# Mixer B's class maxima moved behind the window maxima, and a paired write of the class outputs

## The chip, the cores and the metric

One core of a Trainium2 chip runs the whole layer. The metric is the device time of one execution in microseconds (us). The engines are TensorE (PE: matmuls; PEld: its weight loads), VectorE (DVE), ScalarE (ACT), GpSimd (POOL) and SyncE (SP), which issues most of the DMAs. Each engine works off its own list of instructions in order, and semaphores hold an instruction until what it needs is there.

## The reference

The layer is an encoder layer in float32 over 1024 tokens of width 1024: a norm, an input projection, two attention mixers side by side, an output projection with a residual, a mixture of 32 experts (two for each token), and a last norm. The change touches mixer B alone. It has 8 heads of 64 elements, and merges three patterns by their softmax denominators:

```python
DILATED_PATTERNS = ((128, 1), (512, 4), (2048, 16))
for window, dilation in DILATED_PATTERNS:
    o, lse = _dilated_window(q, k, v, window, dilation)   # |key - query| <= window/2, in steps of dilation
    outs.append(o); lses.append(lse)
w = jax.nn.softmax(jnp.stack(lses, axis=0), axis=0)
o = jnp.einsum('pbhs,pbhsd->bhsd', w, jnp.stack(outs, axis=0))
```

Merging by denominators is one softmax over all keys of the three patterns, in which a key that lies in two of them counts twice. So the kernel needs one maximum for each query over everything that it sees.

## The kernel before

**Stages.** The profiled execution runs through: norm, input projection and mixer A (0 to 430 us); mixer B with the first half of the output projection (430 to 663); the second half with the router (to 760); the experts (to 1340); the last norm. Weights are split into a high and a low float32r part and multiplied in three products.

**Mixer B's two kinds of keys.** The second and third pattern together see every key of the query's residue class modulo 4: four classes of 256 tokens. The first pattern sees a window: for each block of 128 tokens a window of 256. Masks are added to the scores and hold the double counts as log 2.

**A head's preparation** (`prepare_b`, L634). `flipped` transposes the head's keys into `k2` [128 x 1024] and the queries into `q2` and, ordered by class, `q2c`, all of them high part over low part. Then come the class maxima (L651 to 658: for each class two matmuls of `q2c` against `k2[:, c::4]`, which is every fourth column of `k2`; VectorE adds the mask and takes the maximum into `mc`, L657), a multiplication that spreads them (`mx`, L663), and the window maxima (L665 to 677, from `q2` against 256 neighbouring columns of `k2`, into `mw`, L676). Between the second and the third pair of windows, at j0 == 4, ScalarE copies the keys into class order (`k2c`, 128 x 1024, written from `by_class(k2)`) and SyncE copies the low half to `k1c` (L669). At the end four small matmuls with `back_m` (L681) bring the class maxima back into token order, five small VectorE instructions (L683 to 688) join the two and write the negative maximum into the query tile `q` (`keep10` in the order below), and eight transposes (L312, 66 rows) make `q1`, which ScalarE evicts and which every score matmul of the head needs.

**A head's attention** (`steps_b`, L693) has eight steps: four classes (`front_c`: scores, L714 and L715; `back_c`: values, L727 to 730, two classes in one PSUM bank) and four pairs of windows (`front_w`, L740 and L741; `back_w`, L768 to 770). `masked` adds the mask (VectorE, L700), takes the exponential (`p`, ScalarE), rounds it (`ph`, ScalarE) and subtracts (`pl`, GpSimd). After every second class ScalarE evicts the bank into the head's output tile `ob` (L732), class by class, every fourth column; VectorE adds the window parts (L772, three for each head), and `divided` transposes (L749) and divides.

**What sets the order.** `attend` (L464) makes the next head's preparation a generator, and advances it three times after each of the eight steps, so 24 times for each head; a `yield` in `prepare_b` is one advance. This is the program's order. The scheduler of the framework then orders each engine's list anew by a time model of its own, so a moved line moves its neighbours too. `k2c` and `k1c` exist once: the next head's copy can only be written when `front_c` of all four classes of the current head is through. PSUM has three banks for `x` (transposes and maxima), two for `b` (scores), and `i0` and `i1` in turn for outputs. `first_half` (L841) runs beside the heads: its matmuls (L837, 192 of 512 columns in all) are work that PE can do while a head waits; in the prediction they are the fill.

Of the kernel before, what the change touches and what calls it, by code (L numbers as in the profile page):

```python
# [13 lines left out]
F32 = mybir.dt.float32  # L14
# [5 lines left out]
OP = mybir.AluOpType  # L20
AX = mybir.AxisListType

P = 128
# [7 lines left out]
NEG = -1e30  # L31
# [22 lines left out]
def _window(j):  # L54

    return min(max(128 * j - 64, 0), S - 256)
# [70 lines left out]
def tile_encoder(ctx, tc, I, out):  # L127
    nc = tc.nc
    V, A, G, T = nc.vector, nc.scalar, nc.gpsimd, nc.tensor

    def act(o, i, f=AF.Copy, **kw):
        A.activation(o, i, f, **kw)  # L132
# [26 lines left out]
    def bank(tag, shape, dt=F32, name=None):  # L159
        tag = next(turn) if tag == "ip" else names.get(tag, tag)  # L160
        pool, n = psum[tag]
        return pool.tile(shape, dt, tag=tag, name=name or f"ps_{tag}", bufs=n)
# [136 lines left out]
    def by_class(t):  # L299

        return t.rearrange("p (i c) -> p c i", c=4)

    def classes(t):

        return t.rearrange("p (c i) -> p c i", c=4)

    def flipped(dst, src, rows, classed=None):

        for b in range(2):
            ps = bank("x", [P, 4, P], F32R)  # L310
            for i in range(4):
                T.transpose(ps[:rows, i], src[:, 4 * b + i], eyer)  # L312
            if classed is not None:
                act(classes(classed[:rows])[:, :, 128 * b:128 * b + 128],
                    by_class(ps[:rows].rearrange("p j i -> p (j i)")))
            if dst is not None:
                act(dst[:rows, 512 * b:512 * b + 512].rearrange("p (j i) -> p j i", j=4), ps[:rows])
            yield
# [61 lines left out]
    for j in range(NT):  # L380
        x, ss, _ = rows_x[j]
# [6 lines left out]
        for b in range(2):  # L388
            ps = bank("x", [P, 4, P])
# [205 lines left out]
    k1c = k1c[0:66]  # L595
# [6 lines left out]
    qst2 = attb.enter_context(tc.tile_pool(name="qst2", bufs=2, side="right"))  # L602
    pp2 = attb.enter_context(tc.tile_pool(name="pp2", bufs=2, side="right"))
    masks = mcon.tile([P, 6, 256], F32, name="masks")
    mask_c, mask_w = masks[:, 0:2], masks[:, 2:6]
    back_m = mcon.tile([P, 4, P], F32, name="back")
    own = small[:, 60:64]
# [10 lines left out]
    def load_v(h, what):  # L618

        for part in range(2 if h < 8 else 0):  # L620
            to, hs = slice(65 * part, 65 * part + 64), slice(64 * h, 64 * h + 64)
            if what == "w":
                nc.sync.dma_start(v_w[:, :, to].bitcast(F32), bv_d[part, :, hs].rearrange("(j p) c -> p j c", p=P))
            else:
                for c in range(4):
                    nc.sync.dma_start(v_c[:, c, :, to].bitcast(F32),
                                      bv_d[part, c::4, hs].rearrange("(t i) d -> i t d", t=2))

    def load_b(h):
        if h < 8:  # L630
            nc.sync.dma_start(k_st.bitcast(F32), bk_d[h])
            nc.sync.dma_start(q_st[h % 2][:, :, 0:192].bitcast(F32), bq_d[h])

    def prepare_b(h, _):  # L634
        k, q = k_st, q_st[h % 2]
        if h == 0:
            load_b(0)
            nc.sync.dma_start(masks, I["masks"])
            nc.sync.dma_start(back_m, I["back"])
            load_v(0, "c")  # L640
            for _ in range(IDLE):
                yield
        k2 = k2s[h % 2]
        yield from flipped(k2, k, P)
        k1 = k1s[h % 2]
        nc.sync.dma_start(k1[0:64].bitcast(F32), k2[64:128].bitcast(F32))
        q2c = q2s[h % 2]
        yield from flipped(q2, q[:, :, 0:128], P, q2c)
        load_b(h + 1)
        mc = qst2.tile([P, 4, 2], F32, name="mc")  # L650
        junk = qst2.tile([P, 256], F32, name="junk", bufs=1)  # L651
        for c in range(4):
            ps = bank("x", [P, 2, 256])
            for t in range(2):
                T.matmul(ps[:, t], q2c[:, 256 * c + P * t:256 * c + P * t + P], k2[:, c::4], start=True, stop=True)
            for t in range(2):
                V.tensor_tensor_reduce(junk, ps[:, t], mask_c[:, t], 1.0, NEG, op0=OP.add, op1=OP.max,  # L657
                                       accum_out=mc[:, c, t:t + 1])
            yield
        mw = qst2.tile([P, NT], F32, name="mw")  # L660

        mx = qst2.tile([P, 4, 4, 2], F32, name="mx")
        V.tensor_tensor(mx, mc[:, :, None, :].to_broadcast([P, 4, 4, 2]),  # L663
                        own[:, None, :, None].to_broadcast([P, 4, 4, 2]), op=OP.mult)
        for j0 in range(0, NT, 2):  # L665
            if j0 == 4:

                act(classes(k2c), by_class(k2))
                nc.sync.dma_start(k1c[0:64].bitcast(F32), k2c[64:128].bitcast(F32))  # L669
            ps = bank("x", [P, 2, 256])  # L670
            for t in range(2):
                w0 = _window(j0 + t)
                T.matmul(ps[:, t], q2[:, P * (j0 + t):P * (j0 + t) + P], k2[:, w0:w0 + 256], start=True, stop=True)
            for t in range(2):
                w = 0 if j0 + t == 0 else 3 if j0 + t == NT - 1 else 1
                V.tensor_tensor_reduce(classes(junk), by_class(ps[:, t]), classes(mask_w[:, w]), 1.0, NEG,  # L676
                                       op0=OP.add, op1=OP.max, accum_out=mw[:, j0 + t:j0 + t + 1])
            yield
        pm = bank("x", [P, 4, 2])
        for c in range(4):  # L680
            T.matmul(pm, back_m[:, c], mx[:, c], start=(c == 0), stop=(c == 3))  # L681
        m = qst2.tile([P, NT], F32, name="m")
        V.tensor_copy(m.rearrange("p (t i) -> p t i", t=2), pm.rearrange("p i t -> p t i"))  # L683
        t = qst2.tile([P, NT], F32, name="negm")
        V.tensor_tensor(m, m, mw, op=OP.max)
        V.tensor_scalar(t, m, -1.0, None, op0=OP.mult)
        V.tensor_copy(q[:, :, 192], t)
        V.tensor_tensor(q[:, :, 193], t, q[:, :, 192], op=OP.subtract)
        q1 = qst2.tile([66, S], F32R, name="q1")
        yield  # L690
        yield from flipped(None, q[:, :, 128:194], 66, q1)
        return k2, k1, q2c, q1

    def steps_b(h, state):
        k2, k1, q2, q1 = state
        st = {}
# [21 lines left out]
        def back_c(c):  # L718
            if c == 0:
                st["o"] = pp2.tile([65, S], F32, name="ob", bufs=1)  # L720
            if c % 2 == 0:
                st["po"] = bank("ip", [P, 2, 256])
            po, cc = st["po"], c % 2
            ph, pl = st["c", c]
            for t in range(2):
                ts = slice(256 * t, 256 * t + 256)
                T.matmul(po[0:65, cc], v_c[:, c, t, 0:65], ph[:, ts], start=(cc == 0 and t == 0), stop=False,  # L727
                         skip_group_check=True)
                T.matmul(po[0:64, cc], v_c[:, c, t, 65:129], ph[:, ts], start=False, stop=False, skip_group_check=True)
                T.matmul(po[0:65, cc], v_c[:, c, t, 0:65], pl[:, ts], start=False, stop=(t == 1), skip_group_check=True)  # L730
            if cc:
                act(st["o"].rearrange("p (i c) -> p c i", c=4)[:, c - 1:c + 1], po[0:65])  # L732

        def front_w(j0):
            if j0 == NT - 2:
# [20 lines left out]
        def back_w(j0):  # L756
# [16 lines left out]
            if j0 == NT - 2:  # L773
                for b in range(2):
                    divided(b)

        return [(lambda c=c: front_c(c), lambda c=c: back_c(c)) for c in range(4)] + \
            [(lambda j=j: front_w(j), lambda j=j: back_w(j)) for j in range(0, NT, 2)]

# [391 lines left out]
    def load_rows(rows):  # L1171

        gathers.append(G.indirect_dma_start(out=x_g, out_offset=None, in_=xn_d[:, :],  # L1173
                                            in_offset=bass.IndirectOffsetOnAxis(ap=rows, axis=0),
                                            bounds_check=S - 1, oob_is_err=False).ins)
        return x_g
# [7 lines left out]
    def rows_in(xg):  # L1184

        st = {"g": bank("b", [P, 512]), "u": bank("c", [P, 512])}
        for b in range(2):
            st["x", b] = bank("a", [P, 4, P])
            for k in range(4):
                T.transpose(st["x", b][:, k], xg[:, (4 * b + k) * P:(4 * b + k + 1) * P], eye)  # L1190
        return st
# [68 lines left out]
    with tc.manual_schedule(engines={mybir.EngineType.PE}):  # L1260
# [6 lines left out]
        st = rows_in(xg)  # L1267
        rows_split(st, 0)
        for e in range(NE):
# [14 lines left out]
            st = coming  # L1284
# [38 lines left out]
    with tc.For_i(0, n, 1) as i:  # L1323
# [13 lines left out]
        st = rows_in(load_rows(rows[:, 0:1]))  # L1337
# [39 lines left out]
```

## Time and profile before

| | us |
|---|---|
| three runs | 1385.99, 1386.30, 1390.66 |
| median | 1386.3 |
| the profiled execution | 1382.04 |
| its span from the first to the last instruction | 1380.4 |
| PE busy in the span | 1287.7 (93%) |
| DVE busy | 1160.4 (84%) |
| ACT busy | 941.9 (68%) |
| POOL busy | 570.5 (41%) |

A busy PE is not PE at its peak: a matmul's time runs from its start to the end of its results, and the next one starts before that. So how close matmuls follow each other is read from start to start. [...]

### The profile page before, as it was taken

What the parts mean: (1) busy time and instruction counts of PE and PEld (TensorE: products, weight loads), DVE (VectorE), ACT (ScalarE), POOL (GpSimd) and SP (SyncE); (2) the same over time, 40 slices, a digit from 0 to 9 for tenths busy, and PEclk for the clock granted to TensorE, in tenths of its full rate; (3) what the DMA queues carried; (4) which work ended last, traced back from release to release, by engine and by line L of the source; (5) the groups of instructions that cost most, each with busy time, mean ns of one, the idle gap of its engine ahead of it and who ended that gap; (6) DMA issues with size and microseconds to landing.
All of it is one profiled execution on the core that took longest, in us unless ns stands there. A gap on an engine that the chain in (4) does not pass through costs nothing. (4 is left out here: it accounts for less than half of the span.)

```text
span 1380.4 us, 22002 instructions
## 1 busy us (share of the span) xinstructions
PE 1287.7 (93%) x7333; PEld 1091.4 (79%) x7333; DVE 1160.4 (84%) x2001; ACT 941.9 (68%) x1390; POOL 570.5 (41%) x557
## 2 busy tenths in 40 slices
PE   5999999999998988999897999999999999999983
PEld 5999788888976877888686788878888888888862
DVE  6788997899868777887687899989999999999976
ACT  5334566655666885776443888878888888888873
POOL 5673566746566563546354611112111111111215
PEclk9999999999999999999997999999999999999997
DMA  7113321222242485567757999999999999999935
GB/s 260 62 39 85 77 69 57 67 59 49 51 135 61 123 182 149 119 145 234 287 189 266 339 373 364 350 344 360 345 368 342 354 353 358 354 347 351 361 92 224
DMA packets 213685, 301.73 MB, mean 219 GB/s; under 512 B 94436, under 2 KB 116068, under 8 KB 213569
## 3 DMA queue, kind: packets, MB, share of 16 engines
q1 hardware_dynamic: 201168, 275.01, 59.5%
q0 software_dynamic: 11968, 24.55, 6.7%
q8 instruction: 58, 0.95, 0.3%
q10 hardware_dynamic: 432, 0.75, 0.3%
q14 instruction: 59, 0.48, 0.1%
HBM read 267.85 MB, written 44.58 MB: 226 GB/s over the span
## 5 line engine op out<-in xcount | busy, mean ns | idle before, releaser
L1173 POOL DMA_INDIRECT o_b<-xn_d,rows x32 | 51.4, 1606 | 323.8 <-PE ps_a L1190 321.1
L141 DVE TENSOR_TENSOR wl<-unit,wh 128x1024 fp32r<-128x1024 f32 x130 | 156.3, 1221 | 19.9 <-ACT wh L132 19.1
L264 PE MATMUL ps_i<-wih,ul 128*128 128x256 f32 x576 | 164.5, 286 | 1.4 <-DVE ul L141 1.4
L262 PE MATMUL ps_i<-wih,uh 128*128 128x256 f32 x576 | 164.1, 285 | 0.9 <-ACT uh L132 0.8
L263 PE MATMUL ps_i<-wil,uh 128*128 128x256 f32 x576 | 163.4, 284 | 0.0
L542 POOL TENSOR_TENSOR psum<-psum,p 128x512 f32<-128x512 f32 x93 | 136.1, 1463 | 63.2 <-ACT p L132 54.8
L132 ACT ACTIVATE wh<-unit 128x1024 fp32r<-128x1024 f32 x130 | 136.6, 1062 | 34.7 <-PE ps_b L1206 12.5
L132 ACT ACTIVATE ph<-p 128x512 fp32r<-128x512 f32 x192 | 118.6, 633 | 12.0 <-DVE pl L458 5.7
L458 DVE TENSOR_TENSOR pl<-p,ph 128x512 fp32r<-128x512 f32 x93 | 98.3, 1057 | 23.9 <-ACT ph L132 23.7
L132 ACT ACTIVATE p<-ps_b 128x512 f32<-128x512 f32 x128 | 74.9, 596 | 62.1 <-PE ps_b L532 39.1
L262 PEld LDWEIGHTS ps_i<-wih,uh 128*128 128x128 f32 x576 | 111.0, 193 | 7.3 <-ACT uh L132 1.7
L263 PEld LDWEIGHTS ps_i<-wil,uh 128*128 128x128 f32 x576 | 110.9, 193 | 5.7
L264 PEld LDWEIGHTS ps_i<-wih,ul 128*128 128x128 f32 x576 | 111.0, 193 | 5.3 <-DVE ul L141 1.9
L705 POOL TENSOR_TENSOR pl<-p,ph 128x512 fp32r<-128x512 f32 x64 | 86.5, 1365 | 64.3 <-ACT ph L132 57.1
L141 DVE TENSOR_TENSOR wl<-rawc,wh 128x1024 fp32r<-128x1024 f32 x80 | 96.3, 1221 | 11.0 <-ACT wh L132 10.0
L132 ACT ACTIVATE wh<-rawc 128x1024 fp32r<-128x1024 f32 x80 | 84.4, 1062 | 20.8 <-PE ps_b L1206 8.7
L1243 POOL DMA_INDIRECT y_d<-y,rows x31 | 49.9, 1611 | 115.6 <-ACT y L132 112.3
L513 DVE TENSOR_REDUCE m<-ps_x 128x1 f32<-128x512 f32 x128 | 84.8, 678 | 7.9 <-PE ps_x L512 7.6
L1206 PE MATMUL ps_b<-wh,x_hi 128*128 128x512 f32 x256 | 86.5, 419 | 0.0
L1230 PE MATMUL ps_d<-wh,h_hi 128*128 128x512 f32 x256 | 81.0, 397 | 1.7 <-ACT h_hi L132 1.7
L1230 PE MATMUL ps_d<-wh,h_lo 128*128 128x512 f32 x256 | 81.1, 398 | 1.5 <-DVE h_lo L141 1.5
L1206 PE MATMUL ps_b<-wl,x_hi 128*128 128x512 f32 x256 | 81.3, 399 | 0.0
(323 smaller groups left out, 3864.1 us busy)
## 6 DMA issues: line engine op xcount, KB each, us to landing
unit<-in_w_up SPq DMA_DIRECT2D x47, 512.0 KB, 11.8
unit<-in_w_gate SPq DMA_DIRECT2D x42, 512.0 KB, 12.2
unit<-in_w_down SPq DMA_DIRECT2D x41, 512.0 KB, 12.1
rawc<-in_w_gate SPq DMA_DIRECT2D x30, 512.0 KB, 12.1
rawc<-in_w_down SPq DMA_DIRECT2D x26, 512.0 KB, 12.1
rawc<-in_w_up SPq DMA_DIRECT2D x24, 512.0 KB, 11.7
h_b<-in_w_down SPq DMA_DIRECT2D x19, 512.0 KB, 12.8
raw<-in_w_in SPq DMA_DIRECT2D x36, 256.0 KB, 2.9
```

Of the source, the lines that this page charges most:

```text
L132: A.activation(o, i, f, **kw)
L141: (eng or V).tensor_tensor(lo, src, hi, op=OP.subtract)
L262: T.matmul(ps[:, jj], u_hi[j][:, k], wh, start=(k == 0 and jj == 0), stop=False, skip_group_check=True)
L263: T.matmul(ps[:, jj], u_hi[j][:, k], wl, start=False, stop=False, skip_group_check=True)
L264: T.matmul(ps[:, jj], u_lo[j][:, k], wh, start=False, stop=(k == 7), skip_group_check=True)
L458: engine("pl").tensor_tensor(pl, p, ph, op=OP.subtract)
L513: V.tensor_reduce(m2[:, j, b:b + 1], ps, axis=AX.X, op=OP.max)
L542: engine("s").tensor_tensor(st["s"], st["s"], p, op=OP.add)
L705: G.tensor_tensor(pl, p, ph, op=OP.subtract)
L1173: gathers.append(G.indirect_dma_start(out=x_g, out_offset=None, in_=xn_d[:, :], in_offset=bass.IndirectOffsetOnAxis(ap=rows, axis=0), boun ...
L1206: T.matmul(st["gu"[n % 2]], lhs[:, k % 4], rhs[:, 512 * a:512 * a + 512], start=(k == 0 and i == 0), stop=(k == 7 and i == 2))
L1230: T.matmul(py[b], lhs[:, k], w[n][:, 512 * b:512 * b + 512], start=(k == 0 and i == 0), stop=(k == 3 and i == 2))
```

## The change

The window maxima come first. Then, for all heads but the first, the generator gives three advances away, so that the copy into `k2c` still stands behind the current head's last class in the program. Then come the copy and its DMA, and after them the class maxima, which now read 256 neighbouring columns of `k2c` and no longer every fourth of `k2`. `mx` comes after them. No arithmetic is added or taken away, and every engine has as many instructions as before. The eviction of two classes (`act(st["o"]...)`) writes, for each token of the class, both classes' values next to each other, and reads PSUM in that order: in turn from one class's half of the bank and from the other's.

```diff
         mc = qst2.tile([P, 4, 2], F32, name="mc")
         junk = qst2.tile([P, 256], F32, name="junk", bufs=1)
-        for c in range(4):
-            ps = bank("x", [P, 2, 256])
-            for t in range(2):
-                T.matmul(ps[:, t], q2c[:, 256 * c + P * t:256 * c + P * t + P], k2[:, c::4], start=True, stop=True)
-            for t in range(2):
-                V.tensor_tensor_reduce(junk, ps[:, t], mask_c[:, t], 1.0, NEG, op0=OP.add, op1=OP.max,
-                                       accum_out=mc[:, c, t:t + 1])
-            yield
         mw = qst2.tile([P, NT], F32, name="mw")
-
-        mx = qst2.tile([P, 4, 4, 2], F32, name="mx")
-        V.tensor_tensor(mx, mc[:, :, None, :].to_broadcast([P, 4, 4, 2]),
-                        own[:, None, :, None].to_broadcast([P, 4, 4, 2]), op=OP.mult)
         for j0 in range(0, NT, 2):
-            if j0 == 4:
-
-                act(classes(k2c), by_class(k2))
-                nc.sync.dma_start(k1c[0:64].bitcast(F32), k2c[64:128].bitcast(F32))
             ps = bank("x", [P, 2, 256])
             ...
             yield
+
+        for _ in range(3 if h else 0):
+            yield
+        act(classes(k2c), by_class(k2))
+        nc.sync.dma_start(k1c[0:64].bitcast(F32), k2c[64:128].bitcast(F32))
+        for c in range(4):
+            ps = bank("x", [P, 2, 256])
+            for t in range(2):
+                T.matmul(ps[:, t], q2c[:, 256 * c + P * t:256 * c + P * t + P], k2c[:, 256 * c:256 * c + 256],
+                         start=True, stop=True)
+            for t in range(2):
+                V.tensor_tensor_reduce(junk, ps[:, t], mask_c[:, t], 1.0, NEG, op0=OP.add, op1=OP.max,
+                                       accum_out=mc[:, c, t:t + 1])
+            yield
+
+        mx = qst2.tile([P, 4, 4, 2], F32, name="mx")
+        V.tensor_tensor(mx, mc[:, :, None, :].to_broadcast([P, 4, 4, 2]),
+                        own[:, None, :, None].to_broadcast([P, 4, 4, 2]), op=OP.mult)
         pm = bank("x", [P, 4, 2])
...
             if cc:
-                act(st["o"].rearrange("p (i c) -> p c i", c=4)[:, c - 1:c + 1], po[0:65])
+                act(st["o"].rearrange("p (i c) -> p i c", c=4)[:, :, c - 1:c + 1],
+                    po[0:65].rearrange("p c i -> p i c"))
```

The lists of the engines move at three places. In the rows below the number behind a name is that of the buffer: `keep2` is `k2c`, `keep7` the next head's `k2`, `keep8` its `q2c`, `keep1` its `q2`, `keep10` the query tile. The lines of the changed kernel are two or three higher.

**PE in the middle of a head's attention** (the head whose transposes start at 563.5 us), around the first two classes' values, before:

```order
L655 MATMUL ps_x_7007<-keep7_5006,keep8_5007 128x256 x2
L727 MATMUL ps_i0_6995<-ph_6884,v_c_5022 65x256
L729 MATMUL ps_i0_6995<-ph_6884,v_c_5022 64x256
L673 MATMUL ps_x_7015<-keep7_5006,keep1_5000 128x256 x2
L730 MATMUL ps_i0_6995<-pl_6886,v_c_5022 65x256
L727 MATMUL ps_i0_6995<-ph_6884,v_c_5022 65x256
L729 MATMUL ps_i0_6995<-ph_6884,v_c_5022 64x256
L730 MATMUL ps_i0_6995<-pl_6886,v_c_5022 65x256
L727 MATMUL ps_i0_6995<-ph_6926,v_c_5022 65x256
```

and in the changed kernel (L657 is now the window maxima, L671 the class maxima, L832 the fill's transposes):

```order
L657 MATMUL ps_x_7008<-keep7_5006,keep1_5000 128x256 x2
L729 MATMUL ps_i0_6996<-ph_6884,v_c_5022 65x256
L731 MATMUL ps_i0_6996<-ph_6884,v_c_5022 64x256
L832 MATMUL ps_x_7026<-mats_60,on_7018 128x128 x4
L732 MATMUL ps_i0_6996<-pl_6886,v_c_5022 65x256
L729 MATMUL ps_i0_6996<-ph_6884,v_c_5022 65x256
L731 MATMUL ps_i0_6996<-ph_6884,v_c_5022 64x256
L732 MATMUL ps_i0_6996<-pl_6886,v_c_5022 65x256
L671 MATMUL ps_x_7054<-keep2_5001,keep8_5007 128x256 x2
L729 MATMUL ps_i0_6996<-ph_6926,v_c_5022 65x256
```

The first pair of class maxima now stands between the first class's values and the second's, where the second pair's maxima need the copy `keep2`; the eight maxima ahead of the values are now the window's.

**ACT from the eviction of `q1` to the copy `k2c`** in the same head, before:

```order
L132 ACTIVATE p_6881<-p_6881 128x512
L132 ACTIVATE keep8_5007<-ps_x_6956 128x4x128
L132 ACTIVATE keep1_5000<-ps_x_6956 128x512
L132 ACTIVATE p_6923<-p_6923 128x512
L132 ACTIVATE ph_6884<-p_6881 128x512
L132 ACTIVATE keep2_5001<-keep7_5006 128x1024
L132 ACTIVATE p_6987<-p_6987 128x512
L132 ACTIVATE ph_6926<-p_6923 128x512
```

and in the changed kernel:

```order
L132 ACTIVATE p_6881<-p_6881 128x512
L132 ACTIVATE keep8_5007<-ps_x_6956 128x4x128
L132 ACTIVATE keep1_5000<-ps_x_6956 128x512
L132 ACTIVATE p_6923<-p_6923 128x512
L132 ACTIVATE ph_6884<-p_6881 128x512
L132 ACTIVATE p_6988<-p_6988 128x512
L132 ACTIVATE keep2_5001<-keep7_5006 128x1024
L132 ACTIVATE ph_6926<-p_6923 128x512
```

The copy stands one exponential later, and the rounding of the second class (`ph_6926`) comes right behind it.

**DVE at the end of that head**, where the next head's maximum is made, before:

```order
L683 COPY m_7104<-ps_x_7099 128x8
L676 ISA junk_6966,mw_7012<-ps_x_7071,masks_5019 128x256
L676 ISA mw_7012 128x1
L685 TENSOR_TENSOR m_7104<-m_7104,mw_7012 128x8
L686 TENSOR_SCALAR negm_7106<-m_7104 128x8
L687 CAST keep10_5009<-negm_7106 128x8
L688 TENSOR_TENSOR keep10_5009<-negm_7106,keep10_5009 128x8
L772 TENSOR_TENSOR ob_6994<-ob_6994,ps_i0_7161 65x4x112
L864 TENSOR_TENSOR h_b_6008<-ps_d_7570,x2_7389 128x512
L772 TENSOR_TENSOR ob_6994<-ob_6994,ps_i1_7195 65x4x128
L772 TENSOR_TENSOR ob_6994<-ob_6994,ps_i0_7258 65x4x80
```

and in the changed kernel:

```order
L679 TENSOR_TENSOR mx_7119<-mc_6965,mats_60 128x32
L867 TENSOR_TENSOR h_b_6001<-ps_d_7570,x2_7372 128x512
L685 COPY m_7126<-ps_x_7121 128x8
L775 TENSOR_TENSOR ob_6995<-ob_6995,ps_i0_7161 65x4x112
L687 TENSOR_TENSOR m_7126<-m_7126,mw_6967 128x8
L775 TENSOR_TENSOR ob_6995<-ob_6995,ps_i1_7195 65x4x128
L688 TENSOR_SCALAR negm_7128<-m_7126 128x8
L689 CAST keep10_5009<-negm_7128 128x8
L775 TENSOR_TENSOR ob_6995<-ob_6995,ps_i0_7258 65x4x80
L690 TENSOR_TENSOR keep10_5009<-negm_7128,keep10_5009 128x8
```

All three window additions into `ob` now stand ahead of the last instruction of the maximum, where before they stood behind it.

## Rows read from the trace of the kernel before

**Rows 1.** The page, busy time: engine, us, share of the span, instructions.

```profile
PE 1287.7 (93%) x7333; PEld 1091.4 (79%) x7333; DVE 1160.4 (84%) x2001; ACT 941.9 (68%) x1390; POOL 570.5 (41%) x557
```

**Rows 2.** Busy time by windows: from:to, length, PE, PEld, DVE, ACT, POOL, PEclk, DMA, GB/s.

```profile
428.00:660.00 232.00, 211.42 (x1404) 183.88 (x1404) 180.95 (x500) 161.14 (x274) 125.71 (x121) 0.94 0.57 144
...
501.50:537.80 36.30, 31.71 (x201) 26.94 (x199) 26.79 (x72) 21.64 (x37) 16.42 (x16) 0.91 0.74 173
537.80:563.50 25.70, 24.86 (x167) 21.14 (x165) 19.68 (x56) 17.83 (x30) 13.08 (x13) 1.00 0.44 124
563.50:587.00 23.50, 22.38 (x162) 19.74 (x163) 20.58 (x60) 17.95 (x30) 12.17 (x12) 1.00 0.63 146
587.00:609.80 22.80, 21.32 (x157) 19.69 (x156) 19.32 (x59) 17.93 (x30) 11.48 (x11) 0.93 0.59 139
609.80:632.80 23.00, 20.06 (x150) 17.34 (x147) 18.56 (x58) 16.89 (x27) 11.31 (x10) 1.00 0.71 178
632.80:663.00 30.20, 29.88 (x190) 25.85 (x190) 19.63 (x43) 17.55 (x32) 17.48 (x26) 1.00 0.69 218
780.00:1300.00 520.00, 517.28 (x2397) 420.03 (x2396) 473.63 (x461) 436.70 (x512) 97.61 (x67) 1.00 1.00 355
```

**Rows 3.** Groups by form, 428 to 660 us: shapes, count | busy, mean ns | idle before.

```profile
L132 ACT ACTIVATE keep<-ps_x 128x512 fp32r<-128x512 f32 x42 | 23.2, 600 | 8.0 <-PE ps_x L312 7.6
L655 PE MATMUL ps_x<-keep,keep 128*128 128x256 f32 x64 | 20.0, 417 | 0.5 <-DVE mc L657 0.3 <-ACT q L132 0.2
...
L132 ACT ACTIVATE ob<-ps_i 65x512 f32<-65x512 f32 x16 | 17.5, 1091 | 4.3 <-PE ps_i L730 4.3
L132 ACT ACTIVATE keep<-keep 128x1024 fp32r<-128x1024 f32 x7 | 14.6, 2085 | 0.0
L673 PE MATMUL ps_x<-keep,keep 128*128 128x256 f32 x64 | 14.2, 305 | 0.5 <-DVE mc L657 0.3
```

**Rows 4.** PE in order of time: start, us, line, operands, count, [idle before].

```profile
569.00 1.09 PE L655 MATMUL ps_x<-keep,keep 128*128 128x256 f32 x4
569.91 0.30 PE L740 MATMUL ps_b<-keep,keep 128*128 128x256 f32 x1
...
573.37 0.33 PE L727 MATMUL ps_i<-ph,v_c 128*65 128x256 f32 x1 [0.88 <-ACT ph L132]
...
579.90 0.40 PE L673 MATMUL ps_x<-keep,keep 128*128 128x256 f32 x2
580.13 0.28 PE L730 MATMUL ps_i<-pl,v_c 128*65 128x256 f32 x1
```

**Rows 5.** ACT in order of time, the same head.

```profile
564.04 1.08 ACT L132 ACTIVATE q<-ps_x 66x512 fp32r<-66x512 f32 x2 [2.00 <-PE ps_x L312]
...
569.16 0.65 ACT L132 ACTIVATE p<-p 128x512 f32<-128x512 f32 x1
...
570.20 2.08 ACT L132 ACTIVATE keep<-keep 128x1024 fp32r<-128x1024 f32 x1
...
572.69 1.15 ACT L132 ACTIVATE ph<-p 128x512 fp32r<-128x512 f32 x2
```

**Rows 6.** DVE in order of time, the end of the same head.

```profile
582.43 0.17 DVE L683 COPY m<-ps_x 128x8 f32<-128x8 f32 x1
...
583.80 1.18 DVE L688 TENSOR_TENSOR keep<-negm,keep 128x8 fp32r<-128x8 f32 x1
584.90 0.96 DVE L772 TENSOR_TENSOR ob<-ob,ps_i 65x448 f32<-65x448 f32 x1
```

**Rows 7.** Two windows of the next head, columns as in Rows 2.

```profile
594.00:597.00 3.00, 1.62 (x8) 0.80 (x7) 1.97 (x10) 3.00 (x5) 1.23 (x1) 0.99 1.15 303
597.00:600.40 3.40, 3.31 (x16) 3.31 (x17) 3.15 (x12) 2.07 (x4) 3.40 (x4) 0.51 0.83 135
```

**Rows 8.** PE's waits, 428 to 663 us: who <- whom: us, times, longest.

```profile
PE ps_x L312 <- DVE keep L688: 2.8, 3, 1.3
...
PE ps_i L768 <- ACT ob L132: 1.5, 1, 1.5
```

## The prediction

> **What bounds the kernel now.** I read the page's busy times first: PE is busy 93% of the span [rows 1], so PE work is worth having, if it is saved where PE sets the pace. Second the windows [rows 2]. In the experts' stretch, 780 to 1300 us, PE is busy 517.3 of 520 us at a clock of 1.00: it follows on whatever comes before it, so a gain or a loss in mixer B reaches the end undiminished, as long as the weights' transfers keep ahead, and PE's few empty microseconds there say that they do. In mixer B, 428 to 660, PE is busy 211.4 of 232 us: 20.6 us are empty, and they are not spread evenly. The six windows from 501.5 to 663 are cut where PE begins the transposes that make a head's `q1`; I call each a turn. The last turn is filled (29.9 of 30.2), the turns from 587.0 and 609.8 have 1.5 and 2.9 us empty.
>
> Inside a turn I take the one from 563.5. It has two halves. In the **first half** ScalarE sets the pace: it evicts `q1` from 564.04, works through evictions and exponentials, copies `k2c` from 570.20 for 2.08 us and only then rounds the second class, in the pair of `ph` that starts at 572.69 [rows 5]; PE waits 0.88 us for that `ph` and resumes at 573.37 [rows 4]. So the first half is 573.4 - 563.5 = 9.9 us whatever PE does. In the **second half**, 573.4 to 587.0 or 13.6 us, PE goes through values, window scores, maxima and fill, and sets the pace itself.
>
> **The class maxima's matmuls.** Reading every fourth column costs: 64 matmuls at 417 ns mean against 305 ns for the window maxima's 64, of the same shape [rows 3]. From start to start, four of the first take 569.91 - 569.00 = 0.91 us, so 0.23 each; two of the second take 580.13 - 579.90 = 0.23, so 0.115 each [rows 4]. The change gives the class maxima neighbouring columns: 64 x 0.115 = 7.4 us less PE work, or 7.2 by the means. For each head that is 0.92 us, and the question is in which half it falls. Before, the eight class maxima stand in the first half, where ScalarE sets the pace. After, the eight window maxima stand there, and the class maxima, now at 0.115, stand where the window maxima stood at 0.115. So the second half is no shorter, and the first gets 0.92 us more room that ScalarE doesn't give back.
>
> **What else moves between the halves.** The order shows that about eight of the 24 window value matmuls, which before followed `q1`'s transposes and filled the first half, now precede them: 8 x 0.115 = 0.9 us into the second half. Four transposes of `ob` go the same way (0.3 us by PE's pace for short matmuls, an estimate from the 0.115), four of the fill's transposes come the other way (-0.4). PE's empty time in the first half becomes 0.88 + 0.92 + 0.9 + 0.3 - 0.4 = 2.6 us. The copy comes one exponential later (0.65 us, [rows 5]), with the class's rounding right behind it, so PE resumes 0 to 0.6 us later; I take 0.2, since an exponential leaves from behind the copy.
>
> **The end of a head.** Before, the joining runs from 582.43 to the end of the last of its five instructions at 584.98, and `ob`'s next addition starts behind it [rows 6]. After, two or three of these additions stand ahead of its last instruction, 0.96 us each by that row. Also `mx` and the back multiplication follow the last class maximum, where before they were ready early. On the turn from 563.5 the second half then is 13.6 + 0.8 of moved work, and the additions leave `q1`'s transposes 0 to 1 us behind PE's own work. With the later resumption: 23.5 becomes 24.5.
>
> The same bookkeeping for the other turns needs the fill, in blocks of twelve matmuls of 512 columns, at 0.23 each 2.8 us for a block. By the order the turns from 501.5 on hold 36, 36, 24, 12, 12 and 72 of these before, and 48, 24, 24, 24, 24 and 48 after; the sum is the same. A turn with 24 comes out at 24.4 or 24.5, by the turn that I worked out. So: from 501.5, 12 more, of which half goes into that turn's 4.6 empty us [rows 2]: +1.4. From 537.8, 12 fewer, but the ends of the head lie bare: 25.7 to 24.9, -0.8. From 563.5: +1.0. From 587.0: 22.8 to 24.4, +1.6. From 609.8: 23.0 to 24.4, +1.4. The last turn is all PE's, and loses 24 of fill (5.6) and some values: -6.1. Sum -1.5 us.
>
> **The heads before 501.5** share the engines with mixer A. Waits of PE for the maximum, 2.8 us in three [rows 8], get longer by up to `mx` and the back multiplication in series; I take +0.5 (bounds 0 and +3). Their strided maxima give something back where PE is short of time: -0.5 (bounds -2 and 0).
>
> **The eviction in pairs.** Before: 1091 ns for 512 elements, 16 times [rows 3]. What is slow there is one side. The evictions of the transposes, of which a third read PSUM at every fourth element too and write SBUF in a row, take 600 ns mean for 512 [rows 3]; the copy `k2c`, which reads SBUF at every fourth element, takes 2085 for 1024. So a spread on the SBUF side doubles the time and one on the PSUM side costs nothing. Pairs lie between; bounds 0.60 and 1.09, and I take 0.65, nearest to the evictions with a spread PSUM side. That takes 16 x 0.44 = 7.0 us off ScalarE, nearly all of it in second halves, where it has time. PE waited for it once, 1.5 us [rows 8]: -0.5 on the path.
>
> [...]
>
> **Sum.** -1.5 + 0.5 - 0.5 - 0.5 = -2.0 us. The profiled execution took 1382.0 us (span 1380.4), 4.3 below the median of the three runs; it becomes 1380, and the median 1386.3 becomes 1384. A measurement of this kernel can tell about 0.5%, or 6.9 us, from no change.
>
> **Rivals.**
> *PE's saving arrives in full.* If PE, not ScalarE, paces the first halves, the 7.4 us come through, and the pairs' 0.5: -8, so 1378, just over 0.5% faster. For it: PE is busy 91% of the stage [rows 2], and the scheduler's fill may sit better than I read it. Against: PE stands waiting for ScalarE in the very half that the saving falls in [rows 4].
> *Slower: the room in the first halves lets the clock fall.* [...] A fall of 3.4 us takes 1.7 us of PE's work. With 2.6 us empty in each first half this can come in every turn; before, of the turns from 537.8 to 663, one shows a mean clock under 1.00 [rows 2]. Five falls are 8.5 us; with the additions' bound of 1 us more in each of three turns: -2 + 8.5 + 3 = +9.5, so 1396. It is slower by over 0.5% from about six falls' worth, or five with the additions.
> [...]
>
> **How the numbers follow.** Forecast 0.57, full saving 0.25, clock 0.15, pairs as before 0.03. Small parts of the first two cases lie across the 0.5% line: faster 0.24, same 0.60, slower 0.16. The range reaches to 1375, a full saving with both early bounds (-8 and -2, and one clock fall fewer), and to 1394, short of all five falls.
>
> **What the profile after would show.** Right: L671 at about 300 ns mean; the `ob` evictions near 0.65 us; PE waiting for `ph` or the copy in the first halves, 2 to 3 us in each turn; `q1`'s transposes waiting for L690; turns near 24.5 us from 563.5 on and a last turn near 24. [...] What would make it wrong most easily is that ScalarE's chain in the first half shortens by itself, since fewer of PE's values now stand between the transposes that ScalarE evicts; then the first half is not the fixed 9.9 us that I take it for.

## The result: slower by 0.7%

The changed kernel takes 1394.96 us in the median of 16 runs, the kernel before 1386.01 in as many: a ratio of 1.0073, 95% interval 1.006 to 1.0087. That is 9 us slower, past the 0.5% that tell a change from none. The forecast was 1384 and no change, and its range ended at 1394.

### The profile page after: what moved, and what is told of

The parts are those of the page before. It is cut to its first block, busy times and chain, and to the rows that moved or that the text cites. A ratio compares the mean times of both kernels' runs of the same rounds, so it can differ in the third digit from the quotient of the medians.

```text
span 1392.7 us, 21999 instructions
## 1 busy us (share of the span) xinstructions
PE 1290.1 (93%) x7333; PEld 1090.6 (78%) x7333; DVE 1158.3 (83%) x2001; ACT 936.5 (67%) x1390; POOL 568.1 (41%) x557
## 5 line engine op out<-in xcount | busy, mean ns | idle before, releaser
L132 ACT ACTIVATE wh<-unit 128x1024 fp32r<-128x1024 f32 x130 | 136.7, 1062 | 33.3 <-PE ps_b L1209 11.1
L458 DVE TENSOR_TENSOR pl<-p,ph 128x512 fp32r<-128x512 f32 x93 | 92.7, 998 | 26.0 <-ACT ph L132 26.0
L1209 PE MATMUL ps_c<-wh,x_hi 128*128 128x512 f32 x256 | 81.0, 397 | 0.0
```

Of the source, the lines that this page charges most:

```text
L458: engine("pl").tensor_tensor(pl, p, ph, op=OP.subtract)
L1209: T.matmul(st["gu"[n % 2]], lhs[:, k % 4], rhs[:, 512 * a:512 * a + 512], start=(k == 0 and i == 0), stop=(k == 7 and i == 2))
```

## The profile after

The profiled execution took 1394.31 us, 12.3 more than the one before. The page, span and busy time, columns as in [rows 1]:

```profile
span 1392.7 us, 21999 instructions
PE 1290.1 (93%) x7333; PEld 1090.6 (78%) x7333; DVE 1158.3 (83%) x2001; ACT 936.5 (67%) x1390; POOL 568.1 (41%) x557
```

PE is busy for 2.4 us more, although its class maxima became cheaper. To find the place I cut the stage where `q1`'s transposes begin, as in [rows 2]. First the kernel before, for the two turns that run beside mixer A and that [rows 2] don't show one by one (from:to, length, PE, PEld, DVE, ACT, POOL, PEclk, DMA, GB/s; PEclk is the TensorE clock that was granted, as a share of its full speed):

```profile
448.77:474.03 25.26, 23.63 (x155) 21.53 (x155) 19.15 (x53) 22.16 (x38) 16.32 (x12) 0.86 0.37 95
474.03:501.55 27.52, 23.49 (x169) 20.20 (x170) 21.90 (x63) 22.74 (x39) 18.86 (x17) 0.93 0.74 161
```

The changed kernel, the same two turns and then the six that answer to those from 501.5 on:

```profile
449.24:481.86 32.62, 27.43 (x174) 22.66 (x174) 24.90 (x57) 24.60 (x44) 22.00 (x16) 0.87 0.27 73
481.86:514.84 32.98, 26.03 (x166) 22.11 (x165) 20.52 (x62) 19.69 (x34) 15.42 (x14) 0.81 0.69 157
514.84:549.50 34.66, 31.81 (x200) 27.49 (x198) 26.50 (x72) 20.26 (x35) 14.65 (x15) 0.91 0.64 167
549.50:575.18 25.68, 23.96 (x161) 20.75 (x159) 19.29 (x54) 17.26 (x30) 13.13 (x13) 0.93 0.44 123
575.18:600.37 25.19, 23.20 (x172) 20.05 (x170) 20.13 (x62) 16.94 (x30) 12.54 (x12) 1.00 0.54 139
600.37:624.58 24.21, 22.12 (x164) 19.61 (x162) 19.73 (x58) 17.04 (x30) 12.38 (x12) 1.00 0.57 140
624.58:649.76 25.18, 23.66 (x169) 21.27 (x166) 18.98 (x59) 16.91 (x30) 11.41 (x11) 0.93 0.67 178
649.76:674.37 24.61, 23.70 (x158) 20.31 (x155) 16.36 (x34) 16.77 (x29) 14.19 (x21) 1.00 0.76 242
```

The two early turns are 7.4 and 5.5 us longer, 12.8 together. The six later ones sum to 159.5 us, where those from 501.55 to 663.00 took 161.5 before [rows 2]: 1.9 shorter. Both sums end with PE's last instruction before it waits for `on`; up to the first product behind that wait (I call it the next product stage, at 678.59 us, before at 666.14) the six turns take 163.8 us, before 164.6. There the changed kernel is 12.5 us behind, and 12.3 at the end. So the loss stands in the early turns.

The changed groups, 428 to 675 us (shapes, count | busy, mean ns | idle before), answering to [rows 3]:

```profile
L671 PE MATMUL ps_x<-keep,keep 128*128 128x256 f32 x64 | 13.5, 308 | 2.8 <-ACT keep L132 1.4 <-DVE mw L660 1.4
L132 ACT ACTIVATE keep<-keep 128x1024 fp32r<-128x1024 f32 x7 | 14.5, 2073 | 0.0
L132 ACT ACTIVATE ob<-ps_i 65x512 f32<-65x512 f32 x16 | 10.0, 623 | 2.6 <-PE ps_i L732 2.5
```

Both edits do what they say: the class maxima's matmuls went from 417 to 308 ns, the eviction from 1091 to 623. PE's longest waits, 428 to 675 us (who <- whom: us, times, longest), answering to [rows 8]:

```profile
PE ps_i L752 <- DVE ob L775: 4.7, 6, 3.0
...
PE ps_x L683 <- DVE mx L679: 1.9, 3, 0.8
```

Both waits are new: the transposes of `divided` wait for VectorE's last addition, and the back multiplication waits for `mx`. The longest, 3.0 us, is at the end of the first early turn. VectorE there in order of time (start, us, line, operands, [idle before]):

```profile
472.64 0.42 DVE L674 CUSTOM_DVE_ANT_0 junk<-ps_x,masks 128x256 f32<-128x256 f32 x1
472.99 0.08 DVE L674 DVE_READ_ACCUMULATOR2_ANT mc<- 128x1 f32 x1
...
474.19 1.27 DVE L679 TENSOR_TENSOR mx<-mc,mats 128x32 f32<-128x32 f32 x1
475.39 0.99 DVE L775 TENSOR_TENSOR ob<-ob,ps_i 65x448 f32<-65x448 f32 x1
476.62 0.17 DVE L685 COPY m<-ps_x 128x8 f32<-128x8 f32 x1 [0.23 <-PE ps_x L683]
476.82 1.10 DVE L687 TENSOR_TENSOR m<-m,mw 128x8 f32<-128x8 f32 x1
477.95 1.20 DVE L688 TENSOR_SCALAR negm<-m 128x8 f32<-128x8 f32 x1
479.18 1.19 DVE L689 CAST keep<-negm 128x8 fp32r<-128x8 f32 x1
480.28 1.07 DVE L775 TENSOR_TENSOR ob<-ob,ps_i 65x512 f32<-65x512 f32 x1
481.28 0.15 DVE L690 TENSOR_TENSOR keep<-negm,keep 128x8 fp32r<-128x8 f32 x1
```

And PE and GpSimd at the same time:

```profile
477.98 0.41 PE L716 MATMUL ps_b<-keep,keep 128*128 128x256 f32 x1
481.40 0.70 PE L752 MATMUL ps_i<-mats,ob 65*128 65x65 f32 x4 [3.01 <-DVE ob L775]
481.86 0.78 PE L312 MATMUL ps_x<-eyer,keep 128*66 128x128 f32 x5
...
476.62 1.27 POOL L458 TENSOR_TENSOR pl<-p,ph 128x512 fp32r<-128x512 f32 x1
477.85 1.27 POOL L707 TENSOR_TENSOR pl<-p,ph 128x512 fp32r<-128x512 f32 x1
479.07 1.26 POOL L542 TENSOR_TENSOR psum<-psum,p 128x512 f32<-128x512 f32 x1
```

From the end of the last class maximum, 473.07, to `q1`'s transposes, 481.86, it is 8.8 us: two other VectorE instructions, `mx`, the back multiplication, five joining instructions and two additions into `ob`, one behind the other. Three of the five take 1.1 to 1.2 us for 128 x 8 elements, where the first and the last take 0.17 and 0.15: each ends within 0.04 us of a GpSimd instruction's end (477.92 and 477.89, 479.15 and 479.12, 480.37 and 480.33). In the other seven heads all five take 0.14 to 0.25 us. I call the way from the last maximum to `q1` the **tail**. In the same way, from the end of the last maximum's read-out to the start of the transposes, for the eight heads (us):

| kernel | tails | mean |
|---|---|---|
| before | 2.2, 4.2, 6.1, 4.0, 3.1, 4.1, 6.1, 3.1 | 4.1 |
| changed | 3.3, 8.8, 7.0, 5.9, 7.4, 7.4, 6.5, 7.8 | 6.8 |

Before, `mx` ran 5 to 9 us ahead of the last (window) maximum, so the tail was the joining alone, and what VectorE did between its instructions.

The tails don't add up to the loss turn by turn. The first early turn ends with a tail that is 4.6 us longer and grew by 7.4; the second with one that is 0.8 longer and grew by 5.5. In the second the last maximum itself ends 26.0 us into the turn, before 21.4.

## The experiments

All ratios are against the kernel before on the same chip. Letters name theories as they came: A, the preparation ends three advances later; B, the class maxima wait for the copy and a chain follows them, wherever the preparation ends; C, the pairs; D, eight maxima and not four stand behind the copy; E, the tail; H, the maxima's place beside mixer A's work, whoever waits for them.

**Each part alone.** The eviction in pairs alone (e1_pairs), the order alone (e2_order):

```diff
-                act(st["o"].rearrange("p (i c) -> p c i", c=4)[:, c - 1:c + 1], po[0:65])
+                act(st["o"].rearrange("p (i c) -> p i c", c=4)[:, :, c - 1:c + 1],
+                    po[0:65].rearrange("p c i -> p i c"))
```

> The kernel before, with the eviction in pairs alone. Theory A (in the two turns beside mixer A, 449 to 515 us, the head's preparation ends later, with its last steps in series on VectorE; the pairs have no part in the loss): 1385.5 us, that is 0 to 1 less than before, with the 16 evictions at 0.62 us in place of 1.09. Theory C (the faster eviction shifts the order of ScalarE's and PE's lists, and that costs the time): 1393 or more.

> The changed kernel, with the eviction class by class as before (1.09 us). Theory A: 1395 to 1396, as slow as the changed kernel. Theory C (the pairs cost it): 1387, the loss is gone.

The pairs alone: 1382.91 us, ratio 0.9977 (0.9956 to 0.9997), with the eviction at 623 ns. The order alone: 1396.51, 1.0081 (1.0053 to 1.0109). The loss is the order's, and C falls.

**The place.** e3_late: `if h >= 3:` around the new order, the old one in the `else`.

> The changed kernel, but heads 0 to 2, whose preparations run beside mixer A, take their maxima in the old order; heads 3 to 7 in the new one. Theory A: the 12.8 us of the two turns are gone and the rest stays as it was after the change (-1.9 us over the six later turns), so 1382 to 1384. If the loss sits in the new order wherever it stands, and the early turns only show it first: 1390 or more.

1388.49, 1.0022 (1.0003 to 1.004). The turn that answers to 501.5 began at 499.44 us, in the changed kernel at 514.84: the early loss is gone. But the later heads lose something of their own (168.7 us in the trace up to the next product stage, before 164.6), so the expected 1382 to 1384 was missed: by the ratios about two thirds of the loss sit in the early heads, a third in the later.

**Lateness.** e4_idle1 gives one advance away, and e7_late is the kernel before with three given away behind the window maxima:

```diff
-        for _ in range(3 if h else 0):
+        for _ in range(1 if h else 0):
...
+        for _ in range(3 if h else 0):
+            yield
         pm = bank("x", [P, 4, 2])
```

> The changed kernel with one advance given away before the copy in place of three; the copy still stands behind the current head's last class in the program, and a preparation ends one advance later than before the change, not three. Theory A, if it is the lateness that costs: two thirds of the 12.8 us come back, 1386 to 1388. Theory B (the class maxima wait for the copy, and mx and the back multiplication stand in series behind them, wherever the preparation ends): 1394 to 1396, as the changed kernel.

> The kernel before, in which every head but the first gives three advances away between its last window maximum and the back multiplication: the preparation ends as late in the program as in the changed kernel, with nothing else moved. Theory A (lateness alone): the turns from 448 and 474 us grow by some 5 us each, time 1392 to 1397. Theories D and E: they grow by under 2 us each, time 1385 to 1389.

One advance: 1403.44, 1.0127 (1.0097 to 1.0158), slower still, which neither A nor B expected. Three advances in the old order: 1386.41, 1.0001 (0.9981 to 1.0021). So giving advances away costs nothing by itself; but in e7 the scheduler left the back multiplication where it was (20.0 us into the turn, before 19.9), so it says nothing on a later tail. Why e4 is slower than the changed kernel stays open: its profiled execution, 1396.7, was the shortest of its five, so its trace doesn't show the rest.

**The exchange alone.** e5_swap: the kernel before with the two loops exchanged; the class maxima still read `k2[:, c::4]`, the copy stays at its advance.

```diff
+        for j0 in range(0, NT, 2):
...
         for c in range(4):
+            if c == 2:
+                act(classes(k2c), by_class(k2))
...
-        for j0 in range(0, NT, 2):
```

> The kernel before with the two loops of maxima exchanged and nothing else: the window maxima first, then the class maxima, which still read every fourth column of k2 and so need no copy; the copy stays at its advance, now between the second and the third class, and no advance is given away. Theory D (the copy comes at a fixed place, some 9.5 us into a turn, and the new order puts eight maxima and not four behind it; beside mixer A that work finds no room): four maxima stand behind the copy as before, so the turns from 448 and 474 us stay within 2 us of 25.3 and 27.5, and the time is 1385 to 1389. Theory E (mx, the back multiplication and the joining in series on VectorE at the preparation's end): these two turns are still some 5 us longer each, and the time is 1392 to 1397.

1394.26, 1.0067 (1.004 to 1.0094): the whole loss, without a wait for the copy, without an advance given away, without pairs. D falls. The early turns:

```profile
446.92:472.97 26.05, 24.67 (x153) 21.12 (x154) 19.73 (x52) 21.29 (x38) 15.16 (x11) 0.88 0.33 92
472.97:505.85 32.88, 27.70 (x185) 24.53 (x184) 26.23 (x68) 24.22 (x42) 22.07 (x19) 0.87 0.63 158
```

The first grew by only 0.8 us, where E expected some 5, the second by 5.4, and the tails are 2.5, 9.3, 5.6, 6.6, 7.4, 7.8, 7.8 and 5.4, mean 6.5. The profiled execution took 1398.21 us. It is 6.6 us behind the kernel before at the next product stage (672.7), half of the changed kernel's 12.5; the rest of its 16 comes behind mixer B, where no line of the two kernels differs. So the exchange alone gives the loss in the median, and its trace shows half of it in mixer B.

**The disputed saving.** e8_cheap gives the old order the cheap read:

```diff
-                T.matmul(..., k2[:, c::4], start=True, stop=True)
+                T.matmul(..., k2[:, 256 * c:256 * c + 256], start=True, stop=True)
```

> The kernel before, in its old order, but the class maxima read 256 neighbouring columns of k2 in place of every fourth (so the class maxima are those of other keys; the work is the same in all else). It prices the disputed saving by itself. If ScalarE sets the pace where these matmuls stand, as the prediction has it: 1384 to 1387, no change, with the matmuls at 300 ns and PE's empty time up by some 6 us. If PE sets it: 1377 to 1380, the 7 us arrive.

1385.27, 1.000 (0.9981 to 1.0019). Its class maxima, and the turn that answers to 563.5 in [rows 2]:

```profile
L655 PE MATMUL ps_x<-keep,keep 128*128 128x256 f32 x64 | 15.0, 326 | 1.2 <-DVE mc L657 0.8 <-ACT q L132 0.4
563.41:586.95 23.54, 22.23 (x163) 19.37 (x163) 20.64 (x60) 17.94 (x30) 12.16 (x12) 1.00 0.65 146
```

The matmuls are 5 us cheaper in sum (20.0 to 15.0), and the turn takes 23.54 us where it took 23.50. Over 428 to 660 us PE is busy 208.2 us, before 211.4 [rows 2], so its empty time grew by 3.3, less than the 6 expected. The saving falls into PE's waiting, as the prediction had it.

**mx moved in the text.** e9_mxlast puts the lines of `mx` behind the window maxima and changes nothing else.

> The kernel before, with mx (the multiplication that spreads the class maxima) moved behind the window maxima, so that it stands in series before the back multiplication and the joining, as in the changed kernel. Theory E: the turns from 448 and 474 us grow by 3 us or more each, time 1390 to 1396. Theory D: under 1.5 us each, 1385 to 1388.

1383.69, 0.9985 (0.9968 to 1.0003). This didn't test E: `mx`'s inputs are ready early, and the scheduler put it back. In the second early turn it runs before most window maxima, as it did before:

```profile
486.25 0.41 DVE L673 CUSTOM_DVE_ANT_0 junk<-ps_x,masks 128x256 f32<-128x256 f32 x1
486.59 0.08 DVE L673 DVE_READ_ACCUMULATOR2_ANT mw<- 128x1 f32 x1
486.59 0.18 DVE L677 TENSOR_TENSOR mx<-mc,mats 128x32 f32<-128x32 f32 x1
```

So the dependence itself had to be moved, in both directions.

**The tail taken out of the new order** (e10_nodep, the first piece of the diff, from the changed kernel) **and put into the old one** (e11_dep, the second piece, from the kernel before, with `mx` behind the window maxima):

```diff
-        V.tensor_tensor(m, m, mw, op=OP.max)
-        V.tensor_scalar(t, m, -1.0, None, op0=OP.mult)
+        V.tensor_tensor(t, mw, mw, op=OP.max)
+        V.tensor_scalar(t, t, -1.0, None, op0=OP.mult)
...
-                        own[:, None, :, None].to_broadcast([P, 4, 4, 2]), op=OP.mult)
+                        mw[:, None, 4:8, None].to_broadcast([P, 4, 4, 2]), op=OP.max)
```

> The changed kernel with every instruction kept, but the joining takes the maximum from the window maxima alone (the class maxima, their spreading, the back multiplication and its copy still run, and nobody uses them, so the exponentials' offset leaves the class part out). So the head's q and q1 no longer wait behind the last class maximum. Theory E (what costs is the chain at the preparation's end, last class maximum, mx, back multiplication, joining, ahead of q1): the loss is gone, 1382 to 1387, with the turns from 449 and 482 us back to 25 to 29. Theory H (what costs is where the class maxima's matmuls and VectorE's maxima stand, beside mixer A's, whoever waits for them): 1391 to 1396.

> The mirror of it: the kernel before, old order of the two loops, but mx is made behind the window maxima and takes the larger of a class maximum and a window maximum in place of the product with the mask, so it must wait for the last window maximum (the exponentials' offset is larger than needed; no instruction more or less). Now the old order has the same chain at the preparation's end: last maximum, mx, back multiplication, joining. Theory E: 1390 to 1396, with the turns from 449 and 474 us some 3 us or more longer each. Theory H: 1384 to 1388.

Taken out: 1386.17, 1.0023 (0.9999 to 1.0047). Put in: 1391.94, 1.0053 (1.003 to 1.0077). The early turns without the tail, then those of the old order with it:

```profile
450.63:479.25 28.62, 26.15 (x160) 22.25 (x161) 22.61 (x55) 24.00 (x43) 17.39 (x13) 0.86 0.31 83
479.25:503.29 24.04, 21.32 (x162) 19.29 (x163) 19.85 (x60) 19.76 (x35) 16.92 (x17) 0.93 0.74 176
...
448.23:474.38 26.15, 24.81 (x154) 21.81 (x154) 19.78 (x53) 22.26 (x38) 14.39 (x12) 0.83 0.33 91
474.38:505.56 31.18, 27.23 (x182) 23.42 (x182) 25.90 (x66) 23.52 (x40) 21.06 (x19) 0.88 0.69 167
```

Without the tail they sum to 52.7 us, as before (52.8); with it in the old order to 57.3. Both medians came out as E said, and neither as H. e10 takes away more than the tail: `q1` no longer waits for the class maxima at all, so not for the copy either. e11 adds the tail by itself, with nothing given away and no wait for the copy.

By place E did worse. With the tail put in, each early turn was to grow by 3 us or more: the first grew by 0.9, the second by 3.7. And the tail that got longer is that of the first early turn, in e11 (7.7 us, before 4.2) as in e5 (9.3), while the second has one no longer than before (6.0 and 5.6, before 6.1). So these runs show that the dependence costs the time, and not in which turn it is paid. Each edit also lets the scheduler order the lists anew; that this gives all of it is unlikely, since taking out, putting in and (below) shortening all go the way of the tail, but it isn't excluded.

**A shorter joining**, in the changed kernel (e12_short), and in the old order with the pairs (e13_best):

```diff
-        V.tensor_copy(m.rearrange(...), pm.rearrange("p i t -> p t i"))
-        t = qst2.tile([P, NT], F32, name="negm")
-        V.tensor_tensor(m, m, mw, op=OP.max)
-        V.tensor_scalar(t, m, -1.0, None, op0=OP.mult)
-        V.tensor_copy(q[:, :, 192], t)
-        V.tensor_tensor(q[:, :, 193], t, q[:, :, 192], op=OP.subtract)
+        V.tensor_tensor(m.rearrange(...), pm.rearrange("p i t -> p t i"), mw.rearrange(...), op=OP.max)
+        V.tensor_scalar(q[:, :, 192], m, -1.0, None, op0=OP.mult)
+        V.scalar_tensor_tensor(q[:, :, 193], m, -1.0, q[:, :, 192], op0=OP.mult, op1=OP.subtract)
```

> The changed kernel with the joining in three VectorE instructions in place of five (the maximum reads PSUM, the negation rounds straight into q, the rest is one multiply and subtract), with the same result. Theory E: the chain is shorter by two instructions for each head, 0.17 us each where VectorE is free and up to 1.2 each where it took as long beside GpSimd, so 1388 to 1393. Theory H: 1394 to 1396.

> The kernel before with the eviction in pairs and the joining in three instructions; the order of the maxima stays old. Theory E: the joining is on the path here too, but with only 2 to 6 us from last maximum to q1, so 1379 to 1383. Theory H: 1382 to 1384, as with the pairs alone.

e12: 1385.83, 1.0003 (0.9982 to 1.0023): two small instructions fewer for each head take the whole loss back, more than E's 1388 to 1393. Its early turns:

```profile
447.63:477.19 29.56, 26.74 (x162) 22.56 (x162) 22.43 (x53) 24.01 (x43) 19.81 (x15) 0.86 0.29 81
477.19:505.48 28.29, 22.54 (x166) 19.88 (x167) 21.04 (x59) 20.20 (x35) 16.95 (x16) 0.91 0.75 183
```

They sum to 57.9 us, 7.8 less than in the changed kernel and still 5.1 more than before; the six later turns, up to the next product stage, take 160.5, 4.1 less than before. So not all of it comes back where it was lost. The end of the first early turn:

```profile
475.55 0.14 DVE L685 TENSOR_TENSOR m<-ps_x,mw 128x8 f32<-128x8 f32 x1
475.73 0.19 DVE L687 TENSOR_SCALAR keep<-m 128x8 fp32r<-128x8 f32 x1
475.95 1.19 DVE L688 SCALAR_TENSOR_TENSOR keep<-m,keep 128x8 fp32r<-128x8 f32 x1
...
477.19 1.01 PE L312 MATMUL ps_x<-eyer,keep 128*66 128x128 f32 x12 [1.47 <-DVE keep L688]
```

The joining takes 1.6 us here, from 475.55 to 477.14, where the changed kernel needed 4.8 (476.62 to 481.43), an addition of 1.07 among it. e13: 1383.95, 0.9998 (0.9982 to 1.0014), no gain over the pairs alone that shows; E's 1379 to 1383 was missed, and H's number for this run came true. In the old order the joining is not worth shortening. No version here is 0.5% faster than the kernel before; the pairs alone come nearest, with an interval that ends just short of no change.

## Why the prediction was wrong

**The step that failed is "the heads before 501.5".** It gave the chain at a preparation's end +0.5 us (bounds 0 and +3) and took 0.5 off for cheaper reads. Measured: the turns' start that was at 501.55 is at 514.84, 13.3 us later. I had seen the right mechanism, "`mx` and the back multiplication in series", and priced it by PE's waits for the maximum *before* [rows 8], 2.8 us in three. That wait shows what the old tail cost beyond its cover; it is no bound for a tail longer by `mx`, a back multiplication and the additions in between, 2.7 us a head by the table above. Slow small instructions, of which [rows 6] has one at 1.18 us, are not the miss in general: the 40 joining instructions take 9.7 us in the changed kernel and 12.0 before, and three slow ones in a single tail are all that it has. What came on top in the early turns is the clock, below; the prediction feared it for the later turns alone.

**The six later turns were right as a sum, with errors that cancel.** Forecast -1.5, measured -1.9 to PE's last instruction before the wait for `on`, and -0.8 to the next product stage. By turn, forecast and measured: +1.4 and -1.6; -0.8 and -0.1; +1.0 and +1.7; +1.6 and +1.5; +1.4 and +2.1; -6.1 and -5.6. The first is off by 3 us. Why that turn got shorter isn't shown: in e3, where it starts at 499.44, it takes 38.3 us, but in e7, in the old order, 34.9 from 501.28. So the sum was right partly by luck.

**What the profile was to show.** Right: the class maxima near 300 ns (308), the evictions near 0.65 (0.62), turns of 24.2 to 25.2 from 575 on, a last one of 24.6. Wrong: PE's class values wait for `ph` less than before (1.2 us in four waits against 4.0 in five). With their waits for `pl` (3.9 in six, before 1.0 in two) and the maxima's for the copy (1.4 in four) it is 6.5 us over eight heads, and not 2 to 3 in each turn. `q1`'s transposes wait for L690 once, 1.2 us. The new waits stand at the heads' ends.

**The saving is hidden: right**, and it is the forecast's firmest result. 64 maxima got 6.5 us cheaper in sum (20.0 to 13.5; forecast 7.2 to 7.4), and e8 shows that the time doesn't move when they do so in their old place. The rival of the full saving is dead.

**The pairs: right in price, open on the path.** 623 ns against 0.65 forecast; on the path 0.5 us forecast, 3.2 measured by e1's ratio, with an interval from 0.4 to 6.1 that holds both. Reading from the two halves of a bank in turn, ScalarE's eviction took 623 ns, where class by class it took 1091 and the evictions of the transposes take 597. So the case of pairs as before, to which 0.03 was given, is out.

**The clock rival has the right number, 1396, and not the right cause.** It wanted a fall like that of [rows 7], 3.4 us at 0.51, in every later turn; of the six, three have a mean clock under 1.00, where two had before [rows 2]. The falls came in the early turns: the second of them has 0.81, before 0.93. What PE can have lost by that is 0.19 of 32.98 us against 0.07 of 27.52, and in the first turn 0.13 of 32.62 against 0.14 of 25.26: up to 5.0 of the 12.8 us, an estimate from these rows. It follows on the tail and doesn't start the loss: e10, with every instruction kept and the wait taken away, has 0.86 and 0.93, as before. Before and e2 (which has the whole loss), each from 428 us to the third turn and from there to the next product stage:

```profile
428.00:501.55 73.55, 64.26 (x400) 55.29 (x401) 58.37 (x164) 54.07 (x94) 45.30 (x36) 0.88 0.40 93
501.55:666.14 164.59, 150.81 (x1021) 131.12 (x1019) 127.50 (x347) 112.24 (x188) 82.75 (x89) 0.97 0.65 170
...
428.00:514.48 86.48, 67.84 (x418) 55.44 (x418) 63.48 (x170) 54.83 (x95) 47.69 (x38) 0.87 0.35 88
514.48:675.84 161.36, 146.51 (x1009) 126.96 (x1007) 124.95 (x347) 110.54 (x187) 79.54 (x87) 0.98 0.60 167
```

The early stretch is 12.9 us longer at 0.87 against 0.88; PE's empty time in it went from 9.3 to 18.6, and its busy time from 64.3 to 67.8. In the changed kernel's own trace each later turn at 0.93 has lost up to 1.8 us of PE's work, by the same estimate (0.07 of 25.7).

**What stays open.** How the 12.8 us split between the longer wait, the later maxima of the second early turn and the clock. Why e4 is slower than the changed kernel, and how the remaining 0.2% of e10 comes about (its interval reaches to none). That the small instructions are slow because of GpSimd is read from matching ends, not tried by itself.

## What to carry to other kernels

Before exchanging two steps, ask which of them has the longer way to the result that others wait for, and put that one first; here the class maxima need two more steps than the window maxima, and being first had hidden them. Price a serial tail by its steps and by what its engine's list puts between them, not by the waits that the old order left over. Where a scheduler orders the lists, moving a line tests nothing: move the dependence.

## What the runs showed of the hardware

VectorE instructions on 128 x 8 elements take about 0.17 us, or up to 1.3 with their end on the end of a GpSimd instruction. Slow were those with two SBUF operands, a scalar multiplication and a cast (L687, L688, L689 above); the copy and the maximum that read PSUM stayed at 0.13 to 0.18. The 14 traces bear it out: between 405 and 660 us all 106 of them that took over 0.3 us end within 0.06 us of a GpSimd instruction's end, while 52 of the 112 that read PSUM ran from start to end inside one.

A spread of 16 bytes on the SBUF side costs time in three places here: matmuls that read it (417 against 308 ns each; from start to start 0.23 against 0.115 us [rows 4]), evictions that write it (1091 against 623 in pairs), and ScalarE's copy that reads it (2073 for 1024 elements, where a plain rounding of as many takes 1062). On the PSUM side the same spread, which 14 of the 42 evictions of transposes have, cost nothing: one by one these took 582 to 603 ns in the changed kernel, the other 28 took 589 to 611.
